# VectorE scales the residual inside the feed-forward and makes the fillers' low parts; block 2's constants are loaded behind its first projections

## The chip, the cores and the metric

The kernel runs on one core of one Trainium2 chip. The core has five engines that each follow their own instruction order and meet at semaphores: TensorE (PE, matrix products into PSUM; PEld is its weight load), VectorE (DVE), ScalarE (ACT), GpSimd (POOL) and SyncE (SP), which here only issues DMA transfers. The metric is the device time of one execution in microseconds, as the median of several runs.

## What is computed

The reference is two transformer blocks in a row on one sequence of 256 latent tokens and 256 context tokens, width 1024, all in float32. Cut to what matters here:

```python
# block 1: layer 0 a gated linear attention (GLA), layer 1 a state-space mixer (SSD)
hl = layer_norm(ALPHA * hl + m_l[2] * mixer(...), ln_g[i, 0], ln_b[i, 0])
hl = layer_norm(ALPHA * hl + m_l[5] * sq_relu_mlp(modulate(hl, m_l[3], m_l[4]), ffn_w1[i], ffn_w2[i]),
                ln_g[i, 1], ln_b[i, 1])       # in layer 0 also for the context rows hc
# sq_relu_mlp(h, w1, w2) = square(relu(h @ w1)) @ w2, d_ff = 4096
# block 2: two layers, each with three attentions on projections of one normed input
h = rms_norm(x, norm_g[l]) * (1 + scale) + shift
(na_q, na_k, na_v, cq, ckv, ..., z, gm) = split(h @ w_in[l])
x = x + gate * merge_branches(neighbourhood, latent, differential attention)
```

In the feed-forward the normed rows are used twice. Its input is modulated from them, with the gain `ln_g` and bias `ln_b` folded into the modulation's columns; its residual needs them with gain and bias applied: `gain` multiplies the rows by `ln_g` and adds `ln_b` in place.

## The kernel before, in words

**Matrix products in three passes.** Float32 operands are split into a high part (type fp32r) and the low remainder. `gemm` walks over units of weights, 128 x 1024 values (512 KB) each, that `unit` loads: SP issues the transfer into `wr` (three buffers), ScalarE casts it to `wh`, and the subtraction `wl = wr - wh` (line 400) gives the low part; `wh` and `wl` have two buffers each. Which engine subtracts is `self.loeng`: VectorE by default. TensorE then does wh times xh, wh times xl and wl times xh for each output tile.

**Norms and fillers.** Tokens go through a norm in pairs of 128-row tiles. `stats` and `norm` run on VectorE (a chain of 128x2 instructions for the reciprocal root, lines 363 to 371), with one of the two rows scaled on ScalarE; `fill_x` transposes the rows on TensorE and splits them to `xh` and `xl`. While a pair is normed, TensorE is given a product that does not need it, a filler. There are six of them with `lo_on(LOENG)`, four units each, so 24 units: the first 256 columns of the feed-forward's first product in layer 0 (`ffn`, q = c = 0); the first product of the SSD for the first 256 tokens (group 0); the context part of block 2's first projection, computed ahead inside block 1's second feed-forward phase (`nak_ctx`); and in block 2 the first two token tiles of the projections `nav` and `naq` (layer 0) and `nak` (layer 1), by `split=True` in `b_in`. `lo_on` sets `self.loeng` for the product inside it, and sets `self.rate`, the pace of background work (the adaptive modulation, whose accumulations `adav` at line 573 run on VectorE), to 0 if the engine is GpSimd and `keep` is not given. The SSD's product for `z` uses `lo_on(SLO, True)` with `SLO = "gpsimd"`, 16 units more; that line is not touched.

**The feed-forward** (`ffn`) runs over four quarters q of d_ff; in each, two products of the first matrix (c = 0, 1) and two of the second, accumulated in `facc`. The residual `h` is read in the sink of the second product at q = 2. A callback `later` is called after the first product of q = 0.

**The residual's scaling** (`gain`, lines 754 to 761) loads the two rows to all partitions (SP, `row`, four buffers) and does two instructions of 128x1024 per tile, on GpSimd by default (`GAINENG`): four tiles in layer 0 from `later`, two in layer 1 directly ahead of `ffn`. With `after=True` the planner may not put the multiply ahead of the last matmul issued so far.

**Block 2's constants** (`b_consts`): four transfers on SP (`gc`, two parts of `gr`, the lambda vectors in a `bsq` buffer), six small VectorE instructions and one exponential on ScalarE, at the start of each layer.

**Order.** The program's planner (the Tile scheduler with its simulated timeline) fixes each engine's order ahead of the run: among the instructions that it takes to be ready, the one that stands first in the program, moved by `prio`. An instruction may be placed long before its place in the program if its buffers are free. On the chip each engine then follows that order.

Of the kernel before, what the change touches and what calls it, by code (L numbers as in the profile page):

```python
# [22 lines left out]
SRATE = 1  # L23
PEY = 4
VSPLIT = (0,)
LOENG = "gpsimd"
TCN = 4
NBRX = 1
GAH = 1
# [241 lines left out]
class K:  # L271
# [505 lines left out]
    def ffn(self, l, h, u, gates, mode, between=None, later=None):  # L777

        nc, A = self.nc, self.A
        nt = len(h)  # L780
        n = nt * P
        acc = [self.t([P, D], "facc", nt) for _ in range(nt)]
        off1 = off2 = 0
        self.rate = FRATE[l]
        self.wprio = FWP[l]
        for q in range(4):
            hx = self.new_x(mode, 8, n)
            if q == 2:
                gates = gates()
            for c in range(2):  # L790
                def sink(p, k, c0, hx=hx):
                    n = p.shape[1]
                    cs = slice(c0, c0 + n)
                    r = self.t([P, 512], "frelu", 2)
                    nc.scalar.activation(out=r[:, :n], in_=p, func=AF.Relu)
                    if mode == "f4":
                        nc.vector.tensor_tensor(out=hx.h[k][:, cs], in0=r[:, :n], in1=p, op=ALU.mult)
                    else:
                        f = self.t([P, 512], "fsq", 2)
                        nc.scalar.activation(out=f[:, :n], in_=r[:, :n], func=AF.Square)  # L800
                        nc.scalar.copy(out=hx.h[k][:, cs], in_=f[:, :n])
                        nc.vector.tensor_tensor(out=hx.l[k][:, cs], in0=f[:, :n], in1=hx.h[k][:, cs].bitcast(F32),
                                                op=ALU.subtract)
                parts = [(0, n)]
                if q == c == 0 and nt == 4:
                    parts = [(0, 256), (256, 256)]
                for c0, m0 in parts:
                    jobs = [("F", m * P, P, c0, m0, (lambda p, k=c * 4 + m: sink(p, k, c0))) for m in range(4)]
                    with self.lo_on(LOENG if len(parts) == 2 and c0 == 0 else "vector"):
                        o = self.gemm(A[f"w1{l}"], off1, KD, 512, u, jobs)  # L810
                off1 = o
                if later is not None and q == c == 0:
                    later()
            for c in range(2):
                if nt == 4 and 2 * q + c >= FSTOP:
                    self.rate = 0

                def sink2(p, t):
                    cs = slice(c * 512, (c + 1) * 512)
                    a = acc[t][:, cs]  # L820
                    if q == 0:
                        nc.scalar.copy(out=a, in_=p)
                    elif q < 3:
                        nc.vector.tensor_tensor(out=a, in0=p, in1=a, op=ALU.add)
                    else:
                        g = self.t([P, 512], "fsq", 2)
                        nc.vector.tensor_tensor(out=g, in0=p, in1=gates[t][:, cs], op=ALU.mult)
                        nc.vector.tensor_tensor(out=a, in0=a, in1=g, op=ALU.add)
                        self.stats(acc, t, c)
                    if q == 2:  # L830
                        nc.vector.tensor_tensor(out=a, in0=a, in1=gates[t][:, cs], op=ALU.mult)
                        nc.vector.scalar_tensor_tensor(out=a, in0=h[t][:, cs], scalar=ALPHA, in1=a,
                                                       op0=ALU.mult, op1=ALU.add)
                jobs = [("T", 0, 512, t * P, P, (lambda p, t=t: sink2(p, t))) for t in range(nt)]
                if q == 3 and c == 1 and between is not None:
                    self.gemm(A[f"w2{l}"], off2, 8, 512, hx, jobs[:2])
                    between(acc)
                    jobs = jobs[2:]
                off2 = self.gemm(A[f"w2{l}"], off2, 8, 512, hx, jobs)
        self.rate = 0  # L840
        self.wprio = WPRIO
        return acc
# [318 lines left out]
    def ssd(self, u, mode):  # L1161
# [29 lines left out]
        for g in range(8):  # L1191
# [21 lines left out]
            if g == 0:  # L1213
                jobs = [("F", j * P, P, 0, 256, (lambda p, j=j: conv(p, j, 0))) for j in range(3)]
                with self.lo_on(LOENG):
                    self.gemm(A["swin"], off, KD, 512, u, jobs)
# [188 lines left out]
    def block1(self, mode="r3", upto=99):  # L1405
        nc, A = self.nc, self.A
# [22 lines left out]
        u = self.new_x(mode, KD, 512)  # L1429
# [8 lines left out]
        am = {}  # L1438
# [16 lines left out]
        with self.phase("ffn0"):  # L1455
            self.floor = 8
            gl, gc = (self.row_load(d, eng=RLQ) for d in rows)
            xt = load_x("H", RLQ)
            sh, sc = am[0, 3], am[0, 4]
            cols = [self.mod_cols(sh[i], sc[i], 0) for i in (1, 0)]  # L1460
            u = self.new_x(mode, KD, 512)
            r = self.out_resid(A["gwout"], KD, og, xt, [gc, gc, gl, gl],
                               between=lambda r: self.norm_pair(u, r, 0, cols[0]))
            self.norm_pair(u, r, 1, cols[1])
            if upto < 1:
                return
            def gates0():
                gl, gc = (self.row_of(am[0, 5][i]) for i in range(2))
                return [gc, gc, gl, gl]
            u1 = self.X2 = X(mode)  # L1470

            def between0(r):
                self.finish(20)
                sh, sc = am[1, 0], am[1, 1]
                self.cols1 = [self.mod_cols(sh[i], sc[i], 1) for i in (1, 0)]
                self.grow_x(u1, KD, 512)
                self.norm_pair(u1, r, 0, self.cols1[0])
            with self.prio(3000):
                self.ctx_norm()
            r = self.ffn(0, r, u, gates0, mode, between0, lambda r=r: self.gain(r, 0, after=True))  # L1480
            u = u1
            self.norm_pair(u, r, 1, self.cols1[1])
            self.finish(8)
            self.floor = 0
            for t in range(2):
                getattr(nc, Q4).dma_start(out=self.hs[t], in_=r[2 + t])
# [5 lines left out]
        with self.phase("ffn1"):  # L1492
# [17 lines left out]
            u = self.new_x(mode, KD, 512)  # L1510
            self.ctx_to_x(u)
            r = self.out_resid(A["swout"], 16, yx, h, [gl, gl], fac)
# [3 lines left out]
            with self.tc.tile_pool(name="xpf", bufs=1, reuse_waits="tile") as self.xp:  # L1516
                sh, sc = am[1, 3], am[1, 4]
                u = self.new_x(mode, KD, 256)
                self.norm_to_x(u, r, [self.mod_cols(sh[0], sc[0], 2)])
                self.gain(r, 2)  # L1520
                for t in range(2):
                    self.dump(f"h3_{t}", r[t])
                r = self.ffn(1, r, u, lambda: [self.row_of(am[1, 5][0])] * 2, mode)
                self.finish(0)
            self.open_xp2()
            u = self.new_x(mode, KD, 512)
# [45 lines left out]
    def nak_ctx(self, u):  # L1572
# [4 lines left out]
        def sink(p, t):  # L1577
            x = self.t([P, 512], "frelu", 2)
            nc.scalar.copy(out=x, in_=p)
            getattr(nc, Q4).dma_start(out=self.nak0[t], in_=x)  # L1580
        with self.lo_on(LOENG):
            self.b_in(0, "nak", range(2), u, sink)
# [60 lines left out]
    def b_in(self, l, name, toks, u, sink, split=False):  # L1643
# [7 lines left out]
        if not split:  # L1651
            return part(toks)
        with self.lo_on(LOENG):
            part(toks[:2])
        return lambda: part(toks[2:])

    @contextmanager
    def lo_on(self, eng, keep=False):

        old = self.loeng, self.rate  # L1660
        self.loeng = eng
        if eng == "gpsimd" and not keep:
            self.rate = 0
        yield
        self.loeng, self.rate = old
# [455 lines left out]
    def block2(self, mode="r3", upto=99):  # L2121
        nc, A = self.nc, self.A
# [3 lines left out]
        if not hasattr(self, "first2"):  # L2126
            self.open_xp2()
            y, u = [self.ty() for _ in range(4)], self.new_x(mode, KD, 512)
# [6 lines left out]
        with self.phase("b2"):  # L2135
# [6 lines left out]
            for l in range(2):  # L2142
                am = self.am2[l]
                toks = range(4) if l == 0 else range(2, 4)
                self.loeng = B2LO[l]
                ntk = len(toks)
                self.b_consts(l)
                y, u = self.first2 if l == 0 else (ynew, unew)
                t0 = toks[0]
                ya, yb = [x[:, 0:512] for x in y], [x[:, 512:1024] for x in y]  # L2150
# [8 lines left out]
                if l == 0:  # L2159
                    rest2, nav = self.b_v(l, "nav", u, split=True)  # L2160
                    rest3, naq = self.b_qk(l, "naq", toks, u, ya[t0:], 0, split=True)
                    rest()
                    rest2()
                    nak = nak()
                    rest3()
                else:
                    rest()
                    nav = self.b_v(l, "nav", u)
                    nak = nak()
                    naq = self.b_qk(l, "naq", toks, u, ya[t0:], 0)  # L2170
# [160 lines left out]
```

## Time and profile before

| | us |
|---|---|
| median of 3 runs | 2514.3 |
| lowest, highest | 2512.57, 2516.8 |
| profiled execution | 2518.34 |
| its span, first to last instruction | 2516.5 |

The granted clock of TensorE in the profiled execution is 0.973 of full speed on average. PE, DVE, ACT and POOL in the rows are TensorE, VectorE, ScalarE and GpSimd; an engine's busy time does not say whether an instruction was held up while it ran. In a window, PEclk is the mean granted clock of TensorE, 1.00 for 2.4 GHz. The span runs from block 1's GLA over its first feed-forward (from about 405), the SSD (from about 810) and the second feed-forward (from about 1220) to block 2's layer 0 (from about 1436) and layer 1 (from about 2080).

### The profile page before, as it was taken

Reading aid. Unit: us, or ns where it says so; the run is one execution under the profiler, and the core shown is the slowest. Engines: PE = TensorE matmul, PEld = TensorE weight load, DVE = VectorE, ACT = ScalarE, POOL = GpSimd, SP = SyncE. Lnnn points to the kernel's source line nnn. Section 1 sums busy time; section 2 is a strip of 40 time slices with the busy share of each in tenths; the row PEclk is TensorE's granted clock in tenths of the full one; section 3 lists DMA queues with packets and bytes.
Section 4 is the critical chain, followed back from the end, with each engine's and each line's share of the span. In section 5 each row is a group of like instructions: output and inputs, shape, how many; then the busy total and the mean of one; then the engine's idle time right before and its main releaser. Section 6 shows DMA issues by size and latency. Waiting matters only on the chain.

```text
span 2516.5 us, 36824 instructions
## 1 busy us (share of the span) xinstructions
PE 2394.9 (95%) x13879; PEld 1917.3 (76%) x13879; DVE 1741.8 (69%) x3320; ACT 1210.5 (48%) x2367; POOL 363.0 (14%) x308
## 2 busy tenths in 40 slices
PE   7999998999999899999899989999999998999998
PEld 4777766777776777877688868788777877877776
DVE  3455578966588867687765676986555566798676
ACT  3445544432323455565565455554444345564553
POOL 0011113100000134443310120100011001100020
PEclk8999998999999899999999999999999999999999
DMA  6322245555655444523565552222122354333354
GB/s 252 101 77 85 77 148 179 192 200 207 205 199 181 156 161 141 178 84 109 163 209 185 184 172 86 81 80 74 61 92 64 111 168 141 121 111 99 104 154 138
DMA packets 105394, 348.01 MB, mean 138 GB/s; under 512 B 14200, under 2 KB 20288, under 8 KB 105216
## 3 DMA queue, kind: packets, MB, share of 16 engines
q1 hardware_dynamic: 100304, 333.22, 40.4%
q0 software_dynamic: 3616, 12.06, 1.4%
q8 instruction: 109, 1.79, 0.3%
q14 instruction: 69, 0.57, 0.1%
q10 hardware_dynamic: 1296, 0.38, 0.1%
HBM read 338.75 MB, written 6.85 MB: 137 GB/s over the span
## 4 chain that ended last, share of the span: by engine, by line
PE 47%; DVE 3%; ACT 1%; issue 1%; DMA 1%; POOL 0%; SPq 0%; DVEq 0%; POOLq 0%; ACTq 0%
PE acc L439 39%; PE ps L1728 3%; PE ps L1756 2%; PE aps L1867 1%; PE ps L1640 1%; PE aps L1772 1%; DVE wl L400 1%; PE acc L1640 0%; PE ps L741 0%; DMA row<-rowd 0%; DMA bsq<-in_gr 0%; ACT wh L395 0%; DVE xl L751 0%; DVE xl L1718 0%; DVE yacc L1382 0%
## 5 line engine op out<-in xcount | busy, mean ns | idle before, releaser
L395 ACT CAST wh<-wr 128x1024 fp32r<-128x1024 f32 (+3 forms) x461 | 472.5, 1027 | 638.7 <-PE acc L439 557.7
L439 PE MATMUL acc<-wh,xh 128*128 128x512 f32 (+3 forms) x1876 | 727.4, 394 | 12.2 <-ACT wh L395 6.3
L400 DVE TENSOR_TENSOR wl<-wr,wh 128x1024 fp32r<-128x1024 f32 (+3 forms) x421 | 519.2, 1235 | 314.0 <-ACT wh L395 235.4
L439 PE MATMUL acc<-wh,xl 128*128 128x512 f32 (+3 forms) x1876 | 720.4, 388 | 6.7 <-DVE xl L1570 6.4
L439 PE MATMUL acc<-wl,xh 128*128 128x512 f32 (+3 forms) x1876 | 508.0, 387 | 5.8 <-POOL wl L400 4.0
L439 PEld LDWEIGHTS acc<-wh,xh 128*128 128x128 f32 x1876 | 358.3, 192 | 96.7 <-ACT wh L395 12.9
L439 PEld LDWEIGHTS acc<-wh,xl 128*128 128x128 f32 x1876 | 358.5, 192 | 80.6 <-DVE xl L1570 7.7
L439 PEld LDWEIGHTS acc<-wl,xh 128*128 128x128 f32 x1876 | 343.6, 190 | 84.6 <-POOL wl L400 6.2
L439 PE MATMUL acc<-xh,wh 128*128 128x512 f32 (+2 forms) x1024 | 344.3, 353 | 3.8 <-ACT wh L395 2.3
L439 PE MATMUL acc<-xl,wh 128*128 128x512 f32 (+2 forms) x1024 | 340.3, 348 | 7.5 <-DVE xl L751 7.5
L439 PE MATMUL acc<-xh,wl 128*128 128x512 f32 (+1 forms) x1024 | 232.2, 347 | 3.3 <-DVE wl L400 3.3
L439 PEld LDWEIGHTS acc<-xh,wh 128*128 128x128 f32 (+1 forms) x1024 | 196.0, 193 | 38.4 <-issue 6.7
L439 PEld LDWEIGHTS acc<-xl,wh 128*128 128x128 f32 (+1 forms) x1024 | 196.9, 193 | 33.1 <-DVE xl L751 8.8
L400 POOL TENSOR_TENSOR wl<-wr,wh 128x1024 fp32r<-128x1024 f32 x40 | 97.9, 2448 | 720.8 <-ACT wh L395 630.9
L439 PEld LDWEIGHTS acc<-xh,wl 128*128 128x128 f32 x1024 | 167.2, 191 | 36.3 <-issue 6.4
L573 DVE SCALAR_TENSOR_TENSOR adav<-wrd,s,adav 128x512 f32<-128x512 f32 x196 | 146.7, 780 | 53.0 <-DMA wrd<-in_ada 52.0
L1742 ACT ACTIVATE bP<-ps,bnm 128x512 f32<-128x512 f32 (+1 forms) x144 | 88.5, 621 | 86.5 <-DVE bnm L1739 71.4
L2003 POOL TENSOR_SCALAR bP<-bP,brc 128x512 f32<-128x512 f32 (+1 forms) x24 | 33.4, 1396 | 488.2 <-DVE brc L2000 467.5
L1739 DVE TENSOR_REDUCE bnm<-ps 128x1 f32<-128x512 f32 (+1 forms) x120 | 78.2, 684 | 32.3 <-PE ps L1728 32.0
L1204 DVE SCALAR_TENSOR_TENSOR scv<-acc,scw,scv 128x510 f32<-128x510 f32 (+3 forms) x140 | 83.6, 635 | 14.7 <-ACT scv L1200 14.4
L1756 PE MATMUL ps<-ident,bP 128*128 128x128 f32 x400 | 60.3, 277 | 2.5 <-ACT bPT L1631 1.4
L1631 ACT COPY bPT<-ps 128x512 f32<-128x512 f32 x75 | 43.9, 595 | 33.9 <-PE ps L1756 27.9
(430 smaller groups left out, 3100.4 us busy)
## 6 DMA issues: line engine op xcount, KB each, us to landing
wr<-in_w SPq DMA_DIRECT2D x136, 512.0 KB, 3.6
wr<-in_win SPq DMA_DIRECT2D x136, 512.0 KB, 3.6
wrd<-in_ada SPq DMA_DIRECT2D x128, 512.0 KB, 4.4
wr<-in_swin SPq DMA_DIRECT2D x52, 512.0 KB, 3.6
wr<-in_gwin SPq DMA_DIRECT2D x24, 512.0 KB, 3.4
wr<-in_wbr SPq DMA_DIRECT2D x24, 512.0 KB, 3.4
wr<-in_wout SPq DMA_DIRECT2D x24, 512.0 KB, 3.8
wst<-in_ada SPq DMA_DIRECT2D x16, 512.0 KB, 7.3
```

The source lines that it names most:

```text
L395: nc.scalar.copy(out=hi[:, :n], in_=raw[:, :n])
L400: getattr(nc, eng).tensor_tensor(out=lo[:, :n], in0=raw[:, :n], in1=hi[:, :n].bitcast(F32), op=ALU.subtract)
L439: mm = nc.tensor.matmul(out=o, lhsT=wv if kind == "F" else xv, rhs=xv if kind == "F" else wv, start=b["first"], stop=bool(fin and b["left" ...
L573: o = nc.vector.scalar_tensor_tensor(out=a, in0=xi, scalar=c, in1=a, op0=ALU.mult, op1=ALU.add)
L1204: nc.vector.scalar_tensor_tensor(out=c[:, :, o0:o1], in0=pv[:, :, i0:i1], scalar=w[:, tap:tap + 1], in1=c[:, :, o0:o1], op0=ALU.mult, op1= ...
L1631: return self.nc.scalar.copy(out=out, in_=in_)
L1640: nc.tensor.transpose(p[:width, t * P:(t + 1) * P], x[:, j * width:(j + 1) * width], self.ident)
L1728: mms.append(self.nc.tensor.matmul(out=p[:, n * nk:(n + 1) * nk], lhsT=q[a][rows, i * P:(i + 1) * P], rhs=k[b][rows, :nk], start=m == 0, s ...
L1739: nc.vector.tensor_reduce(out=nm[:, :n], in_=p.rearrange("p (n k) -> p n k", n=n), axis=AX.X, op=ALU.max, negate=True)
L1742: nc.scalar.activation(out=e[:, i * nk:(i + 1) * nk], in_=p[:, i * nk:(i + 1) * nk], func=AF.Exp, bias=nm[:, i:i + 1], accum_out=sm[i])
L1756: mms.append(nc.tensor.transpose(p[:, d:d + P], e[:, c:c + P], self.ident))
L2003: nc.gpsimd.tensor_scalar(out=b, in0=b, scalar1=rc[:, 1, i:i + 1], scalar2=None, op0=ALU.mult)
```

## The change

Three edits. `LOENG` becomes "vector", so that the 24 filler units have their low part made by VectorE; `lo_on` now sets the rate to 0 whenever `keep` is not given, and `ffn` passes `keep` for all of its products but the first, so that the rates are those of before. The callback `later` is called at q = 1, c = 0 instead of q = c = 0, and both feed-forwards pass `gain` on VectorE as that callback; in layer 1 it stood ahead of `ffn`. `b_consts` moves from the start of each block-2 layer to a place behind the rest of the projection `nak` (layer 1), or of `nak` and `nav` (layer 0).

```diff
--- before.py
+++ after.py
@@ -23,7 +23,7 @@
 SRATE = 1
 PEY = 4
 VSPLIT = (0,)
-LOENG = "gpsimd"
+LOENG = "vector"
 TCN = 4
 NBRX = 1
 GAH = 1
@@ -806,10 +806,10 @@
                     parts = [(0, 256), (256, 256)]
                 for c0, m0 in parts:
                     jobs = [("F", m * P, P, c0, m0, (lambda p, k=c * 4 + m: sink(p, k, c0))) for m in range(4)]
-                    with self.lo_on(LOENG if len(parts) == 2 and c0 == 0 else "vector"):
+                    with self.lo_on(LOENG, len(parts) == 1 or c0 > 0):
                         o = self.gemm(A[f"w1{l}"], off1, KD, 512, u, jobs)
                 off1 = o
-                if later is not None and q == c == 0:
+                if later is not None and q == 1 and c == 0:
                     later()
             for c in range(2):
                 if nt == 4 and 2 * q + c >= FSTOP:
@@ -1477,7 +1477,7 @@
                 self.norm_pair(u1, r, 0, self.cols1[0])
             with self.prio(3000):
                 self.ctx_norm()
-            r = self.ffn(0, r, u, gates0, mode, between0, lambda r=r: self.gain(r, 0, after=True))
+            r = self.ffn(0, r, u, gates0, mode, between0, lambda r=r: self.gain(r, 0, nc.vector, True))
             u = u1
             self.norm_pair(u, r, 1, self.cols1[1])
             self.finish(8)
@@ -1517,10 +1517,8 @@
                 sh, sc = am[1, 3], am[1, 4]
                 u = self.new_x(mode, KD, 256)
                 self.norm_to_x(u, r, [self.mod_cols(sh[0], sc[0], 2)])
-                self.gain(r, 2)
-                for t in range(2):
-                    self.dump(f"h3_{t}", r[t])
-                r = self.ffn(1, r, u, lambda: [self.row_of(am[1, 5][0])] * 2, mode)
+                r = self.ffn(1, r, u, lambda: [self.row_of(am[1, 5][0])] * 2, mode,
+                             later=lambda r=r: self.gain(r, 2, nc.vector, True))
                 self.finish(0)
             self.open_xp2()
             u = self.new_x(mode, KD, 512)
@@ -1659,7 +1657,7 @@
 
         old = self.loeng, self.rate
         self.loeng = eng
-        if eng == "gpsimd" and not keep:
+        if not keep:
             self.rate = 0
         yield
         self.loeng, self.rate = old
@@ -2144,7 +2142,6 @@
                 toks = range(4) if l == 0 else range(2, 4)
                 self.loeng = B2LO[l]
                 ntk = len(toks)
-                self.b_consts(l)
                 y, u = self.first2 if l == 0 else (ynew, unew)
                 t0 = toks[0]
                 ya, yb = [x[:, 0:512] for x in y], [x[:, 512:1024] for x in y]
@@ -2161,10 +2158,12 @@
                     rest3, naq = self.b_qk(l, "naq", toks, u, ya[t0:], 0, split=True)
                     rest()
                     rest2()
+                    self.b_consts(l)
                     nak = nak()
                     rest3()
                 else:
                     rest()
+                    self.b_consts(l)
                     nav = self.b_v(l, "nav", u)
                     nak = nak()
                     naq = self.b_qk(l, "naq", toks, u, ya[t0:], 0)
```

## Rows read from the trace of the kernel before

**Rows 1.** Page, part 1: the span; busy us, share and instructions of each engine.

```profile
span 2516.5 us, 36824 instructions
PE 2394.9 (95%) x13879; PEld 1917.3 (76%) x13879; DVE 1741.8 (69%) x3320; ACT 1210.5 (48%) x2367; POOL 363.0 (14%) x308
```

**Rows 2.** GpSimd's groups by shape: count, busy us, mean ns, idle before and its releasers.

```profile
L400 POOL TENSOR_TENSOR wl<-wr,wh 128x1024 fp32r<-128x1024 f32 x40 | 97.9, 2448 | 720.8 <-ACT wh L395 630.9 <-PE acc L439 81.5 <-issue 8.0
...
L761 POOL TENSOR_TENSOR yacc<-yacc,row 128x1024 f32<-128x1024 f32 x6 | 17.7, 2983 | 0.0
...
L758 POOL TENSOR_TENSOR yacc<-yacc,row 128x1024 f32<-128x1024 f32 x6 | 15.1, 2540 | 18.8 <-PE ps L741 18.8
```

**Rows 3.** VectorE's groups by shape, the costliest, with the same columns.

```profile
L400 DVE TENSOR_TENSOR wl<-wr,wh 128x1024 fp32r<-128x1024 f32 x392 | 498.1, 1272 | 294.5 <-ACT wh L395 223.7 <-PE acc L439 55.5 <-ACT bsq L2019 5.3
```

**Rows 4.** Source line 758, its VectorE instructions: ns min, median, max, first and last start.

```profile
L758 DVE TENSOR_TENSOR by<-by,row x2: 1218/1222/1226, 1450.2 to 1451.4; 128x1024 f32<-128x1024 f32 x2
```

**Rows 5.** Windows, seven stretches and one for comparison; the first line names the columns.

```profile
core 0: us, PE busy (x) PEld busy (x) DVE busy (x) ACT busy (x) POOL busy (x), PEclk, DMA share, GB/s
404.00:436.00 32.00, 26.18 (x174) 24.20 (x173) 29.32 (x50) 17.74 (x36) 16.21 (x7) 0.84 0.45 149
436.00:458.00 22.00, 14.33 (x70) 12.06 (x69) 22.00 (x18) 8.06 (x19) 15.88 (x6) 0.77 0.33 107
809.00:850.00 41.00, 26.44 (x150) 22.36 (x149) 33.52 (x87) 18.31 (x33) 10.92 (x6) 0.74 0.36 119
1220.00:1248.00 28.00, 19.34 (x74) 13.64 (x73) 21.11 (x47) 12.10 (x18) 10.06 (x5) 0.94 0.56 193
1248.00:1270.00 22.00, 18.14 (x125) 17.27 (x125) 20.09 (x21) 13.09 (x29) 11.33 (x5) 0.84 0.52 169
1436.00:1492.00 56.00, 45.07 (x180) 33.80 (x179) 42.35 (x72) 28.30 (x47) 25.62 (x14) 0.91 0.54 180
2080.00:2120.00 40.00, 33.36 (x140) 25.97 (x139) 28.00 (x47) 23.90 (x45) 10.68 (x6) 0.87 0.44 143
2040.00:2080.00 40.00, 39.31 (x177) 31.25 (x176) 29.21 (x47) 21.46 (x33) 3.26 (x6) 1.00 0.73 229
```

**Rows 6.** Timeline of VectorE: start us, us, instruction, shape, count, idle before if any.

```profile
419.09 2.27 DVE L365 TENSOR_SCALAR rsqy<-rsqy 128x2 int32<-128x2 int32 x1
...
446.82 5.60 DVE L573 SCALAR_TENSOR_TENSOR adav<-wrd,s,adav 128x512 f32<-128x512 f32 x2
...
812.47 2.28 DVE L369 TENSOR_TENSOR rsqw<-rsqy 128x2 f32<-128x2 f32 x1
...
823.16 0.15 DVE L369 TENSOR_TENSOR rsqw<-rsqy 128x2 f32<-128x2 f32 x1
...
1226.92 3.49 DVE L1382 SCALAR_TENSOR_TENSOR yacc<-wrd,yacc 128x512 f32<-128x512 f32 x2
...
1263.03 3.39 DVE L400 TENSOR_TENSOR wl<-wr,wh 128x1024 fp32r<-128x1024 f32 x1
...
1452.49 6.72 DVE L761 TENSOR_TENSOR by<-by,row 128x1024 f32<-128x1024 f32 x2
...
2062.80 1.29 DVE L2239 TENSOR_TENSOR by<-by,bo 128x512 f32<-128x512 f32 x2
...
2086.22 3.16 DVE L2239 TENSOR_TENSOR by<-by,bo 128x512 f32<-128x512 f32 x2
```

**Rows 7.** Timeline of TensorE, two starts after a wait, with the wait in brackets.

```profile
821.65 1.92 PE L586 MATMUL aps<-adav,one 128*32 128x512 f32 x4 [9.48 <-DVE adav L573]
...
2103.88 1.54 PE L741 MATMUL ps<-ident,by 128*128 128x128 f32 x6 [4.15 <-ACT by L1624]
```

**Rows 8.** Windows inside the two feed-forwards, columns as in the windows above.

```profile
540.00:560.00 20.00, 20.00 (x90) 15.16 (x89) 15.61 (x23) 8.36 (x17) 0.00 (x0) 1.00 0.59 201
1310.00:1330.00 20.00, 20.00 (x149) 19.04 (x148) 11.05 (x15) 14.30 (x32) 0.00 (x0) 1.00 0.62 184
```

**Rows 9.** Timeline of SyncE's queue: one transfer of the constants of block 2's layer 1.

```profile
1968.08 0.33 SPq L2107 DMA_DIRECT2D bsq<-in_gr  x1
```

## The prediction

> **What bounds the kernel now.** The page first [rows 1]: TensorE is busy 2394.9 of 2516.5 us, so nothing gains unless it lets TensorE wait less or run at its upper clock; VectorE at 69% and GpSimd (POOL) at 14% matter only where TensorE waits for them. The groups of GpSimd come next [rows 2]: what the change takes from it is 40 low parts minus the 16 that the variable `SLO` keeps, so 24 of 2.45 us, and the scalings of the residual, six multiplies of 2.54 and six additions of 2.98 us. GpSimd has time for both, and TensorE hardly waits for it by name.
>
> The windows say where the time goes [rows 5]. A stretch's loss is its length less TensorE's busy time times the granted clock. It is 10.0 us in 404 to 436, 11.0 in 436 to 458, 21.4 in 809 to 850, 9.8 in 1220 to 1248, 6.8 in 1248 to 1270, 15.0 in 1436 to 1492 and 11.0 in 2080 to 2120, 85 us together. The 24 low parts and the 12 scalings all run in these seven stretches: each is a norm whose latency TensorE bridges with fillers, four units of weights (eight in 1436 to 1492). The stretch 2040 to 2080 is a norm of the same kind, whose fillers' low parts VectorE makes already: TensorE is busy 39.31 of 40 us at full clock.
>
> VectorE's timeline shows the mechanism [rows 6]. Two 128x512 additions take 1.29 us at 2062.80 and 3.16 at 2086.22, while GpSimd makes a low part. An instruction on 128x2 takes 0.15 us at 823.16, 2.28 at 812.47 beside a low part, and 2.27 at 419.09 beside a scaling. So a GpSimd instruction holds VectorE up for most of its own length, in the chain that TensorE waits for: 4.15 us at 2103.88 for the normed rows, 9.48 at 821.65 behind an accumulation of VectorE [rows 7].
>
> The Trainium skill, "SBUF — State Buffer", section "Who interferes with whom", says that the two engines share a port pair by an exclusive lock, held for the whole instruction. By that alone the 36 instructions could block VectorE for 24 x 2.45 + 6 x 2.54 + 6 x 2.98 = 92 us, an estimate; the timeline has 60.6, as VectorE is not always due, and the sum uses that.
>
> **Blocked time, by stretch.** I add what VectorE's instructions took beyond the same shape unblocked; one row of each stretch stands [rows 6]. 404 to 436: six instructions, 9.4 us (5.1 by low parts, 4.3 by scalings). 436 to 458: six, 12.4, all scalings. 809 to 850: three, 7.9. 1220 to 1248: three, 4.5. 1248 to 1270: four, 8.2, all scalings. 1436 to 1492: four, 11.1, where the two additions at 1452.49 alone took 6.72 against 2 x 1.22 [rows 4]. 2080 to 2120: four, 7.1. Low parts block 35.7 us, scalings 24.9.
>
> **Low parts.** 24 go to VectorE at 1.22 us (the unblocked length; the group's mean of 1.27 has blocked ones in it [rows 3]): 29.3 us more work, 35.7 less blocking, a net of only 6.4. Behind a waiting low part on VectorE stand the norm and, behind that, ScalarE's cast of the next weights and TensorE. The mean idle time before a low part is 294.5/392 = 0.75 us [rows 3], mostly where VectorE has nothing else to do; in the norm at 2040 to 2080 the loss is 0.7 us in all, low parts included [rows 5]. Ends: nothing added where VectorE idles, -35.7; every low part waiting 0.75, 29.3 + 18.0 - 35.7 = +11.6. I take the value near the net, as that stretch is the nearest case. GpSimd's remaining work does not shrink: the low parts of `SLO` and the bias additions still block where they stand. The rates of the background work stay as they were, as `lo_on` now sets them to 0 by `keep` and the callers pass it to match.
>
> **Residual scaling, first feed-forward.** Eight instructions leave GpSimd and come back on VectorE at 1.22 us [rows 4], 9.8 us, a pass of weights later (q = 1, c = 0), near 550 us. There TensorE is busy 20.00 of 20 us and VectorE 15.61 [rows 8], so the work fits on average; in one burst it can hold up a low part. 20.00/90 x 24 matmuls make a unit of 5.3 us, one unit is ahead, so a burst costs at most 9.8 - 5.3 = 4.5 us, once. **Second feed-forward:** four instructions, 4.9 us, from just before to q = 1, c = 0, near 1320; VectorE has 11.05 of 20 us there and TensorE waits for nothing [rows 8]. 20.00/149 x 24 = 3.2 us a unit, so at most 1.7. Both: 0 to 6.2 us, I take 2, as other instructions can come in between. The four row loads on SP (512 KB each) move back as well; they stay far ahead of their use and the row buffers suffice, so I give them 0, with 1 us either way where they stand among weight loads. The result is read at q = 2, two gemms later.
>
> **Block 2's constants.** Four transfers, six small VectorE instructions and one ScalarE exponential per layer are placed behind the first projections. The planner issues them when a queue is idle: layer 1's constants were issued at 1968.08 [rows 9], over 100 us before that layer began. So the move may do nothing; layer 0's leave the norm at best. What can go is under 1 us of unblocked instructions, with SP's four issues of 0.43 us up to 3. Their use is tens of us later, behind the projections; no loss.
>
> **Sum.** What reaches TensorE, by stretch: 404 to 436, 9.4 - 4.9 = 4.5. 436 to 458, 12.4 blocked but only 11.0 lost, and VectorE is full there without it (22.00 of 22): 9. 809 to 850, 7.9 - 4.9 = 3.0: 2, since the 9.48 us wait is for an accumulation behind the norm. 1220 to 1248, 4.5 - 4.9: 0. 1248 to 1270, 8.2 blocked, 6.8 lost: 6. 1436 to 1492, 11.1 - 9.8 = 1.3, and with the constants and the low parts that fall before the norm: 3. 2080 to 2120, 7.1 - 4.9 = 2.2, and by its twin at 2040: 3. Together 27.5, less 2 for the bursts: 25.5. The profiled execution took 2518.3 us, so 2492.8; it stands 4.0 above the median of the runs (2514.3), which gives 2489 us.
>
> **Rivals.** A: this forecast, 15 to 40 us less. 0.60.
>
> B: low parts wait in VectorE's queue. If the planner's order has them before their weights are cast, each adds the 0.75 us of the group [rows 3], 18 us: -25.5 + 18 = -7.5, 2507 us. For it: that mean; against: the stretch at 2040. 0.15.
>
> C: more comes back. Idle and lost clock feed each other: in 436 to 458 the clock is 0.77 [rows 5], TensorE at its lower level (1.2 GHz) for part of it right after waits. If half of the 85 us returns, 2472 us. 0.08.
>
> D: no change, within 0.2% (5 us, about what a measurement of this kernel can tell): moving work between two engines that block each other gains nothing, and the planner's new order costs what the scalings give. By rows: low parts +11.6, scalings -17 (three stretches at 4.3, 9 and 6 less 2): -6, about 2509; 2514 with 5 us of order lost. The Trainium skill, "Perfetto Trace Analysis", section "Optimizing Scalar/DVE Operations", says that offloading between these two might not help as they share a read port; the trace bears it out for the low parts (net 6.4 of 60.6), not for the scalings, which go where VectorE idles. 0.10.
>
> E: slower. One mechanism: VectorE works in order, and a low part that stands before a norm's instruction holds it until TensorE frees the weight buffer, one filler unit earlier. From a mean wait of 25.5/24 = 1.1 us per low part the gain is gone; at 1.5 us it is 36 - 25.5 = 10.5 us slower, 2525. For it: a filler unit outlasts that wait; against: rows 5 at 2040 again, and that TensorE has fillers while VectorE waits. 0.07.
>
> **Numbers.** Faster A, B and C, 0.83; same D, 0.10; slower E, 0.07. The range 2470 to 2510 holds A, B, most of C and the near half of D; the ends of the terms (-35.7 - 21.6 - 3, and +11.6 + 6.2) go beyond it on both sides, but would all have to fall together.
>
> **What would show it.** GpSimd's group of low parts has 16 instead of 40, with no multiply or addition of rows on yacc, and VectorE's low parts grow to 416 (of 128x1024). In the seven stretches VectorE's 128x2 instructions take under 0.2 us; TensorE's waits after 436 and at 1263 are gone, and the clock is higher there. The twelve scalings stand near 550 and 1320, and TensorE stays 20 of 20 us busy around them. Wrong would be: a low part on VectorE waiting over 1 us inside a norm, TensorE idle around 550, or new waits in block 2 behind another order. The largest term, 436 to 458, fails if TensorE there waits for VectorE's accumulations anyway.

## The result, and the profile after

The changed kernel takes 2486.69 us (median of 4 runs, 2483.96 to 2490.76), the one before 2513.44 us beside it (median of 4): ratio 0.9894, 95% interval [0.9878, 0.9909], so 23 to 31 us less. Forecast were 2489 us, in 2470 to 2510. The profiled execution took 2490.76 us against 2518.34.

The page of the changed kernel, to be read against [rows 1], then its groups of low parts by shape, against [rows 2, 3]:

```profile
span 2489.0 us, 36804 instructions
PE 2382.5 (96%) x13879; PEld 1908.7 (77%) x13879; DVE 1725.9 (69%) x3356; ACT 1210.8 (49%) x2367; POOL 271.5 (11%) x272
```

```profile
L400 POOL TENSOR_TENSOR wl<-wr,wh 128x1024 fp32r<-128x1024 f32 x16 | 38.1, 2381 | 86.9 <-PE acc L439 72.2 <-ACT wh L395 14.7
...
L400 DVE TENSOR_TENSOR wl<-wr,wh 128x1024 fp32r<-128x1024 f32 x416 | 519.8, 1252 | 298.2 <-ACT wh L395 234.2 <-PE acc L439 42.0 <-ACT xtmp L921 6.8
```

GpSimd loses 24 low parts and all twelve scalings. VectorE has 36 instructions more and is busy 15.9 us less: 36 at 1.22 us, 43.9, came, so by this sum 59.8 us of held-up time went, against the 60.6 that the prediction counted. Windows of the changed kernel, to be read against [rows 5] (the third and fourth at the same work, 22 and 26 us earlier; the fifth around the first scalings, against [rows 8]), and VectorE's timeline of those scalings:

```profile
404.00:433.00 29.00, 24.06 (x170) 22.80 (x169) 23.77 (x53) 18.24 (x35) 0.00 (x0) 0.88 0.52 165
433.00:458.00 25.00, 24.47 (x133) 19.91 (x133) 24.56 (x51) 12.98 (x27) 0.00 (x0) 1.00 0.66 232
...
1226.00:1248.00 22.00, 21.17 (x151) 19.35 (x151) 14.87 (x27) 16.46 (x35) 1.14 (x2) 0.96 0.57 190
...
2054.00:2092.00 38.00, 33.23 (x150) 26.58 (x149) 27.48 (x54) 26.64 (x48) 1.08 (x2) 0.96 0.52 168
530.00:552.00 22.00, 22.00 (x95) 16.83 (x94) 21.72 (x26) 10.80 (x17) 0.00 (x0) 1.00 0.60 198
```

```profile
534.05 4.62 DVE L758 TENSOR_TENSOR yacc<-yacc,row 128x1024 f32<-128x1024 f32 x4
538.59 1.41 DVE L573 SCALAR_TENSOR_TENSOR adav<-wrd,s,adav 128x512 f32<-128x512 f32 x2
539.91 3.49 DVE L761 TENSOR_TENSOR yacc<-yacc,row 128x1024 f32<-128x1024 f32 x3
```

Behind 433 us TensorE is busy 24.47 of 25 us at the upper clock (2.4 GHz), where before it was 14.33 of 22 at 0.77. In the feed-forward VectorE is full for a while (21.72 of 22 us) and TensorE does not notice.

Both traces have 13879 matmuls, so one can ask how much earlier the matmul with the same number starts. That gives the gain of each stretch (times of before; worked out from the starts of the matmuls at both ends of it; us):

```
stretch        forecast  changed   the stretch is
404 to 436        4.5      2.6     norm, low parts and scalings
436 to 458        9       11.5     norm, scalings
809 to 855        2        5.5     norm, low parts
855 to 1220       0       -2.2     SSD stage, nothing of it edited
1220 to 1270      6        5.7     norm, low parts, then scalings
1436 to 1492      3        2.9     norm, low parts, constants
2080 to 2120      3        4.4     norm, low parts
498 to 776       -2       -0.6     first feed-forward, burst of scalings
2120 to the end   0       -2.4     block 2, layer 1
```

The -2 was forecast for the bursts of both feed-forwards; the second shows -0.1. The rest is under 1 us a line. The stretches of the edit gave 32.6 us, 5 of them went again elsewhere, 27.6 are left in these two traces. The -0.6 is not the burst's: it stands in the traces of the runs below that leave the scalings on GpSimd beside the norms and move the low parts of the first feed-forward's head, and it is 0.0 where the scalings alone are moved.

### The profile page after: what moved, and what is told of

The parts are those of the page before. It is cut to its first block, busy times and chain, and to the rows that moved or that the text cites. A ratio compares the mean times of both kernels' runs of the same rounds, so it can differ in the third digit from the quotient of the medians.

```text
span 2489.0 us, 36804 instructions
## 1 busy us (share of the span) xinstructions
PE 2382.5 (96%) x13879; PEld 1908.7 (77%) x13879; DVE 1725.9 (69%) x3356; ACT 1210.8 (49%) x2367; POOL 271.5 (11%) x272
## 5 line engine op out<-in xcount | busy, mean ns | idle before, releaser
L400 DVE TENSOR_TENSOR wl<-wr,wh 128x1024 fp32r<-128x1024 f32 (+4 forms) x445 | 540.8, 1217 | 318.2 <-ACT wh L395 246.6
L573 DVE SCALAR_TENSOR_TENSOR adav<-wrd,s,adav 128x512 f32<-128x512 f32 x196 | 140.3, 747 | 44.8 <-DMA wrd<-in_ada 43.5
L1754 PEld LDWEIGHTS ps<-ident,bP 128*128 128x128 f32 x400 | 45.9, 140 | 16.5 <-issue 5.9
```

Source lines behind the costliest of these rows:

```text
L400: getattr(nc, eng).tensor_tensor(out=lo[:, :n], in0=raw[:, :n], in1=hi[:, :n].bitcast(F32), op=ALU.subtract)
L573: o = nc.vector.scalar_tensor_tensor(out=a, in0=xi, scalar=c, in1=a, op0=ALU.mult, op1=ALU.add)
L1754: mms.append(nc.tensor.transpose(p[:, d:d + P], e[:, c:c + P], self.ident))
```

## The experiments

The theory: a GpSimd instruction holds VectorE up, and what counts is whether TensorE waits for VectorE at that time; the scalings are the larger part. One rival the trace of before settles: ScalarE, which casts the weights, is not held. Its casts of line 395 take 1.05 us in the median beside GpSimd's 128x1024 instructions (20 of them) and 1.05 elsewhere (412). Differences in us below are medians against the kernel before on the same chip; ratios have 95% intervals.

**One part at a time.** First the scalings alone:

```diff
-                if later is not None and q == c == 0:
+                if later is not None and q == 1 and c == 0:
...
-            r = self.ffn(0, r, u, gates0, mode, between0, lambda r=r: self.gain(r, 0, after=True))
+            r = self.ffn(0, r, u, gates0, mode, between0, lambda r=r: self.gain(r, 0, nc.vector, True))
...
-                self.gain(r, 2)
...
+                             later=lambda r=r: self.gain(r, 2, nc.vector, True))
```

> Theory (GpSimd's long instructions hold VectorE up inside the norms that TensorE waits for, and the scalings are the larger part that reaches TensorE): with the scaling edit alone the stretches 436 to 458 and 1248 to 1270 lose their TensorE waits, 404 to 436 gains some, 809 to 850, 1220 to 1248, 1436 to 1492 and 2080 to 2120 stay as before. By the terms 4.3 + 9 + 6 less 2 that is 17 us, 15 to 20 us faster than before. Rival 1 (the low parts carry the gain, since they were most of the blocked time, 35.7 of 60.6 us): 5 to 10 us faster. Rival 2 (the gain is that of a luckier order of the planner as a whole, not the sum of the parts): no fixed number, but the parts alone would not add up to the 27 us of the whole.

2491.49 us, ratio 0.9903 [0.9884, 0.9923], 22.4 us less. The gain falls where the theory had it and is larger than its price: 404 to 458 gains 15.9 us and 1203 to 1273 6.5. Rival 1 is out. So is rival 2 for the first of these: from 404 to 498 TensorE, VectorE and ScalarE do the same instructions in the same order as before. The complement is the whole change without those lines. What it still has, in part:

```diff
-LOENG = "gpsimd"
+LOENG = "vector"
...
-                self.b_consts(l)
...
+                    self.b_consts(l)
```

> The low parts on VectorE and the moved constants, with the scalings on GpSimd at their old places. Theory: 809 to 850 and 2080 to 2120 gain what they gained in the changed kernel (5.6 and 4.3 us), 1436 to 1492 some 3, the stretches beside scalings little, and block 2's other order takes some 2 back: 6 to 12 us faster than before. Rival 1 (low parts carry the gain): 17 us or more. Rival 3 (low parts are neutral, since 24 of 1.22 us come onto VectorE and net out the blocking): within 4 us of before.

2510.24 us, 0.9978 [0.9966, 0.9990], 3.6 us less. Here 776 to 853 gains 5.6, 1203 to 1273 2.8, 1436 to 1492 3.2 and 2080 to 2120 3.5, but the SSD stage (853 to 1203) gives back 6.9 and 404 to 498 loses 2.0. With the 22.4 that is 26.0 of the 26.75 us: the parts add up, against rival 2 of the run before. Then the constants alone:

```diff
-                self.b_consts(l)
                 y, u = self.first2 if l == 0 else (ynew, unew)
...
                     rest2()
+                    self.b_consts(l)
...
                     rest()
+                    self.b_consts(l)
```

> Only the constants of block 2 are placed behind the first projections. Theory: they were issued ahead of need before, so no change, within 1.5 us. Rival: their four issues and seven small instructions stood in the norm of 1436 to 1492, and the move is the 3 us gained there: 2 to 4 us faster.

2514.16 us, 0.9999 [0.9985, 1.0013]: nothing. The rival is out: 1436 to 1492 loses 0.3, so the 2.9 us there are the low parts'.

**Place or engine.** The changed kernel (lines with - are its own from here on) with the late scalings on GpSimd:

```diff
-... lambda r=r: self.gain(r, 0, nc.vector, True))
+... lambda r=r: self.gain(r, 0, nc.gpsimd, True))
...
-                             later=lambda r=r: self.gain(r, 2, nc.vector, True))
+                             later=lambda r=r: self.gain(r, 2, nc.gpsimd, True))
```

> The changed kernel with the scalings at their new, later places, but on GpSimd. It tells the place from the engine. Theory (what cost time was GpSimd's instructions beside the norm; any place where TensorE has work does): as fast as the changed kernel, within 3 us, so 24 to 30 us faster than before; VectorE's instructions beside the scalings in the feed-forward are held up by about 2 us each and TensorE does not notice. Rival (the engine matters: twelve GpSimd instructions of 2.5 to 3.0 us, 33 us together, hold up VectorE's low parts in the feed-forward, where VectorE is 15.6 of 20 us busy): 5 us or more of the gain is lost, 22 us faster than before or less.

2510.53 us, 0.9984 [0.9971, 0.9997], only 3.3 us less. That looks like the rival, but its timelines of GpSimd, and of TensorE beside it, show something else:

```profile
405.29 5.76 POOL L758 TENSOR_TENSOR yacc<-yacc,row 128x1024 f32<-128x1024 f32 x2 [51.34 <-PE ps L741]
431.85 5.16 POOL L758 TENSOR_TENSOR yacc<-yacc,row 128x1024 f32<-128x1024 f32 x2 [20.81 <-PE ps L741]
436.98 11.11 POOL L761 TENSOR_TENSOR yacc<-yacc,row 128x1024 f32<-128x1024 f32 x4
```

```profile
443.38 0.58 PE L439 MATMUL acc<-xl,wh 128*128 128x256 f32 x1 [8.02 <-DVE xl L751]
```

The scalings did not move. GpSimd has an otherwise empty queue there and starts what its data allow, at 405 and 432 us; a later line in the program, and an order kept only within the planner, hold nothing back. So the run doesn't tell place from engine. It shows again what the old place costs: TensorE waits 8.02 us for an `xl` that VectorE makes beside them. The next run holds them truly, by one instruction ahead in GpSimd's queue, beside that edit (a dependency within the planner keeps the scalings behind it):

```diff
                 if later is not None and q == 1 and c == 0:
+                    z = self.t([P, 512], "frelu", 2)[:, :2]
+                    self.hold = nc.gpsimd.tensor_copy(out=z, in_=hx.h[3][:, 0:2].bitcast(F32))
                     later()
```

> The changed kernel with the scalings on GpSimd, and held to their new place this time: ahead of them GpSimd copies two columns of a tile that the feed-forward's second part makes (into a spare tile), and its queue runs in order. Theory 1 (the place is what counts: beside the norm a held-up VectorE is what TensorE waits for, in the feed-forward it is not): 20 to 27 us faster than before, the norms as in the changed kernel. Theory 2 (the engine counts as well: beside 22 us of GpSimd work near 540 VectorE gets one instruction done for each of GpSimd's, 8 where it has 25 due, and falls 11 us behind, more than the 5 us that a unit of weights is ahead): 5 to 12 us are lost in the first feed-forward, fewer in the second, 10 to 18 us faster than before.

2500.12 us, 0.9928 [0.9912, 0.9944], 16.3 us less: theory 2. The norms gain as in the changed kernel (404 to 458: 14.1 us), and 498 to 776 loses 12.6. The window, then the timelines of GpSimd, VectorE and TensorE around the scalings (line 763 is line 761 of the other kernels):

```profile
540.00:560.00 20.00, 14.22 (x54) 9.90 (x52) 17.68 (x11) 4.73 (x6) 16.44 (x7) 0.87 0.30 106
```

```profile
544.15 10.72 POOL L758 TENSOR_TENSOR yacc<-yacc,row 128x1024 f32<-128x1024 f32 x4
554.83 11.98 POOL L763 TENSOR_TENSOR yacc<-yacc,row 128x1024 f32<-128x1024 f32 x4
```

```profile
545.72 6.95 DVE L573 SCALAR_TENSOR_TENSOR adav<-wrd,s,adav 128x512 f32<-128x512 f32 x3 [1.57 <-DMA wrd<-in_ada]
552.59 3.35 DVE L400 TENSOR_TENSOR wl<-wr,wh 128x1024 fp32r<-128x1024 f32 x1
555.87 2.86 DVE L573 SCALAR_TENSOR_TENSOR adav<-wrd,s,adav 128x512 f32<-128x512 f32 x1
558.65 2.57 DVE L571 TENSOR_SCALAR adav<-wrd,s 128x512 f32<-128x512 f32 x1
561.14 3.41 DVE L400 TENSOR_TENSOR wl<-wr,wh 128x1024 fp32r<-128x1024 f32 x1
```

```profile
556.00 2.93 PE L439 MATMUL acc<-xh,wl 128*128 128x512 f32 x6 [5.78 <-DVE wl L400]
```

From 545.72 to 564.55 us VectorE finishes seven instructions, 2.3 to 3.4 us each, about a GpSimd instruction's length. The low parts of the weights come late, and TensorE waits 5.78 us for one; its granted clock in the window is 0.87, where it was 1.00. Even where VectorE has some 4 of 20 us to spare [rows 8], GpSimd is the dear engine for this. The mirror of it, VectorE at the old places:

```diff
-                if later is not None and q == 1 and c == 0:
+                if later is not None and q == c == 0:
...
+                self.gain(r, 2, nc.vector)
...
-                             later=lambda r=r: self.gain(r, 2, nc.vector, True))
```

> The changed kernel with the scalings on VectorE but written at their old places (behind the first gemm of the first feed-forward, and ahead of the second). Theory (a VectorE instruction there costs the norm its own 1.22 us, not the 2 to 3 us of a held-up one): 12 of 1.22 are 14.6 us, of which some fall into VectorE's idle time, so 5 to 12 us of the gain are lost: 14 to 21 us faster than before. Rival (only the engine counts, VectorE's queue has room): as the changed kernel, within 3 us. Rival (only the place counts): 2 to 7 us faster than before, as with GpSimd.

2489.61 us, 0.9893 [0.9875, 0.9912]: as the changed kernel, 2489.39 us beside it. My theory's 5 to 12 us are not there; the first rival is right. The scalings ran beside the norm, and TensorE stayed busy (VectorE's timeline of the first four, then the window):

```profile
440.90 4.62 DVE L758 TENSOR_TENSOR yacc<-yacc,row 128x1024 f32<-128x1024 f32 x4
```

```profile
433.00:458.00 25.00, 23.66 (x122) 19.22 (x121) 25.00 (x37) 12.04 (x26) 0.00 (x0) 1.00 0.49 164
```

VectorE is full for all 25 us, and background accumulations give way: 11 `adav` instructions of line 573 start in it instead of the changed kernel's 21, the rest later. 404 to 498 gains 11.7 instead of 14.7 us, and the first feed-forward then gains another 1.1.

**What VectorE takes on.** The scalings on GpSimd at the old places, and at the new ones twelve VectorE instructions of the same shape that leave the residual as it is:

```diff
+    def idle_work(self, r):
+        for x in r:
+            for _ in range(2):
+                o = self.nc.vector.tensor_tensor(out=x, in0=x, in1=x, op=ALU.max)
+                self.not_before(o)
```

> The changed kernel with the scalings on GpSimd at their old places, beside the norms, and with twelve VectorE instructions of the same shape at the new places that leave the residual as it is (the larger of x and x). It splits the scaling edit into what leaves GpSimd and what VectorE takes on. Theory (the whole gain is what leaves GpSimd, the twelve VectorE instructions are covered by TensorE's full queue): as with the scalings left where they were, 2510 us, 2 to 7 us faster than before. Rival (VectorE's twelve instructions cost up to 4.5 + 1.7 us in bursts, so the removal is worth more than was seen): 2514 to 2518 us.

2510.06 us, 0.9973 [0.9961, 0.9984], 6.4 us less, no slower than without them (3.6 us less, on another chip). The first eight ran from 548.75 to 559.84 us, and the window there:

```profile
545.00:565.00 20.00, 20.00 (x86) 15.24 (x85) 19.51 (x23) 10.82 (x17) 0.00 (x0) 1.00 0.57 180
```

The bursts cost nothing that can be measured. Four runs on one chip, this one among them, give the whole table, in us less than before: GpSimd at the old places 6.4 (this run, with the twelve idle instructions), GpSimd at the new ones 16.3, VectorE at the old 26.8, VectorE at the new 27.0. The engine is worth 20 us at the old places and 11 at the new; the place is worth 10 on GpSimd and nothing on VectorE.

**Single low parts, and noise.** The changed kernel again:

> The changed kernel once more, on the chip of the runs beside it, as their yardstick: 2486.7 us, 25 to 29 us faster than before.

2489.39 us, 0.9885 [0.9864, 0.9905]. Its stretches gain 5.8 (776 to 853), 5.3 (1203 to 1273) and 4.3 us (2080 to 2120), but the SSD stage gives back 4.6 instead of 2.5, and at 404 us this execution is 7 us ahead of the first one of the same program, at its end 1. So much in a single profile's stretch is accident.

The traces also say how far the SSD stage's loss is one of order. In the runs with the scalings alone and with the constants alone, TensorE, VectorE and ScalarE have the order of the kernel before in 853 to 1203; the one loses 3.4 us there all the same, the other gains 3.0. In the seven traces with the changed kernel's order it loses 1.0 to 6.9. The cost of the order shows best in 880 to 950: 4.9 to 11.0 us in those seven, 0.0 and 1.6 in the two. A part comes back behind it, and what the order costs in the whole stage can't be told from one trace. Then the low parts of the SSD stage on VectorE too:

```diff
-SLO = "gpsimd"
+SLO = "vector"
```

> The changed kernel with the last 16 low parts, those of the SSD stage, on VectorE as well. Theory (a low part that moves frees VectorE of about what it costs, 1.22 us on it against some 1.5 us of blocking in a norm, and the SSD stage has other GpSimd work, which stays): no change against the changed kernel, within 4 us; by the low parts' price here (24 of them and the constants gave 3.6 us) 2 us faster. Rival (VectorE is 16 to 22 of 25 us busy in the SSD stage, and its queue holds a low part in front of the scan's own steps): 4 to 10 us slower than the changed kernel.

2495.03 us, 0.9919 [0.9901, 0.9937], 21 us less than before where the changed kernel had 27. By medians that is the rival, some 6 us slower; but the changed kernel was not run on this chip, the interval of its second set of runs, [0.9864, 0.9905], overlaps a little with this one, and the profile, that of the fastest run (2489.13 us), shows no place for a loss. It stays open. Next the four low parts of the first feed-forward's head back on GpSimd:

```diff
-                    with self.lo_on(LOENG, len(parts) == 1 or c0 > 0):
+                    with self.lo_on("gpsimd" if len(parts) == 2 and c0 == 0 else "vector", len(parts) == 1 or c0 > 0):
```

> The changed kernel with the low parts of the first feed-forward's head alone, four units near 404 to 420, back on GpSimd. In the run with the scaling edit alone, where they were on GpSimd, the stretch 404 to 497 gained 17.5 us, against 14.2 in the changed kernel. Theory (there the low parts stand between the norm's 128x2 steps in VectorE's queue and cost what their blocking did, so the place decides for each filler): 2 to 4 us faster than the changed kernel. Rival (the difference of two runs was an accident of a transfer, and four low parts are 5 us on either engine): within 1.5 us of the changed kernel.

2494.66 us, 0.9919 [0.9903, 0.9935], on the same chip: 5 us slower by medians, again at the edge of what the intervals tell apart. The theory's gain is not there in the whole. In the edited stretch it is: 16.5 us gained from 404 to 498 against 14.7. TensorE's first wait for the normed rows there, before, in the changed kernel and in this one:

```profile
424.65 1.54 PE L741 MATMUL ps<-ident,yacc 128*128 128x128 f32 x6 [5.28 <-ACT yacc L723]
```

```profile
424.49 2.46 PE L741 MATMUL ps<-ident,yacc 128*128 128x128 f32 x10 [4.94 <-ACT yacc L723]
```

```profile
420.36 0.87 PE L741 MATMUL ps<-ident,yacc 128*128 128x128 f32 x6 [1.04 <-ACT yacc L723]
```

But 776 to 853 gains 2.7 less, and the SSD stage gives back 10.2 us. Nothing was edited there; the planner's queues for it came out in another order, but this profile is also that of the slowest of six runs (2500.95 us), so how much of it is the order's stays open. The mirror, these four alone on VectorE, on the kernel before:

```diff
-                    with self.lo_on(LOENG if len(parts) == 2 and c0 == 0 else "vector"):
+                    with self.lo_on("vector", len(parts) == 1 or c0 > 0):
...
-        if eng == "gpsimd" and not keep:
+        if not keep:
```

> The mirror of the run before it: the kernel before with the four low parts of the first feed-forward's head alone on VectorE, all else as it was. The changed kernel with these four on GpSimd was 5 to 8 us slower than the changed kernel, and none of that fell in the stretch beside them; it fell between 809 and 1270. Theory (what four low parts give beside the norm is about nothing, 5.1 us of blocking against 4 of 1.22 us; the 5 to 8 us are the queues' new order in the SSD stage, which comes out differently for every edit ahead of it): stretch 404 to 497 within 2 us of before, and the whole within 4 us of before, with a shift of either sign in the SSD stage. Rival (these four low parts are worth 5 to 8 us wherever the time shows): 5 to 8 us faster than before.

2514.87 us, 1.0007 [0.9996, 1.0018], 377 to 498 gains 1.1: beside GpSimd's scalings these four are worth nothing, as the theory had it. Last, the four low parts of the SSD stage's first projection back on GpSimd, in the changed kernel:

```diff
-                with self.lo_on(LOENG):
+                with self.lo_on("gpsimd"):
                     self.gemm(A["swin"], off, KD, 512, u, jobs)
```

> The changed kernel with the four low parts of the SSD stage's first projection alone back on GpSimd. The changed kernel gained 5.7 us in 809 to 855, where 2 had been counted on; the run with the scaling edit alone gained 2.4 there. Theory (these low parts blocked the norm ahead of the SSD stage, and the loss was half idle time and half clock, so taking 7.9 us of blocking away gives more than the 3 us net): the stretch loses 3 to 4 us again, and the whole is 2 to 5 us slower than the changed kernel. Rival (the stretch's gain is one of order): the stretch keeps its 5 us.

2488.19 us, 0.9903 [0.9886, 0.9919]. The stretch (776 to 853) is 7.3 us worse, more than the theory said, and the SSD stage behind it, in another order, gains 3 to 5 of these back. The whole is 2 us slower by medians, which the intervals don't tell from nothing. The rival is out for the stretch. TensorE's timeline in this kernel, then in the changed one ([rows 7] has 9.48 for before):

```profile
805.44 1.92 PE L586 MATMUL aps<-adav,one 128*32 128x512 f32 x4 [9.47 <-DVE adav L573]
...
822.22 0.39 PE L439 MATMUL acc<-xl,wh 128*128 128x256 f32 x1 [1.76 <-DVE xl L751]
```

```profile
805.73 1.92 PE L586 MATMUL aps<-adav,one 128*32 128x512 f32 x4 [7.37 <-DVE adav L573]
```

No version beat the changed kernel; the one with VectorE at the old places equals it.

## Why the prediction was right, point by point

- **The mechanism** held. The chain of 128x2 instructions of the changed kernel, in VectorE's timeline beside four low parts on VectorE (against 2.27 and 2.28 in [rows 6]):

```profile
418.18 0.17 DVE L363 TENSOR_SCALAR rsqy<-lnv 128x2 int32<-128x2 int32 x1
418.38 0.17 DVE L365 TENSOR_SCALAR rsqy<-rsqy 128x2 int32<-128x2 int32 x1
...
420.50 1.22 DVE L400 TENSOR_TENSOR wl<-wr,wh 128x1024 fp32r<-128x1024 f32 x1 [0.58 <-ACT wh L395]
421.64 0.15 DVE L370 TENSOR_TENSOR rsqw<-rsqw,lnv 128x2 f32<-128x2 f32 x1
```

- **404 to 436** was mis-sized: 4.5 forecast, 2.6 measured. The rows above show why: a low part stands inside the chain, with a wait of 0.58 us and 1.22 of its own, and the norm ends at 424 us as before (TensorE's wait there is 4.94 us, against 5.28). Where the scalings are gone and these low parts stay on GpSimd, the stretch gains 4.4 us (scalings alone) and 5.4 (the head's low parts put back) and the wait is 1.04. So the whole gain there is the scalings', and the four low parts cost some 2 us of it.
- **436 to 458**, the largest term, was 9 and gave 11.5: I took off 2 because VectorE is full there. It is full without the scalings as well (24.56 of 25 us), but with background work that can wait, and the granted clock comes back from 0.77 to 1.00.
- **The scalings** were 17 and measured 22.4, interval 19 to 29 less by the ratio: 404 to 458 gains 15.9 where 13.3 was reckoned, and the bursts cost nothing where 2 was taken.
- **Low parts and constants** were 8.5 and measured 3.6 by medians (2.5 to 8.5 less by the ratio). Behind the first feed-forward they gave more than forecast: in the three runs with the low parts moved and GpSimd's scalings beside the norms, 776 to 853 gains 4.9 to 5.6 against 2. I had taken off 1 because TensorE's wait there was for an accumulation behind the norm; that accumulation stood behind held-up instructions itself, and in the changed kernel the wait falls from 9.48 to 7.37 us. The other 3 us come later in the stretch, at a granted clock that the sum had no term for. Windows of about the same work, before and then in the changed kernel:

```profile
844.00:855.00 11.00, 8.88 (x49) 8.12 (x50) 5.35 (x13) 3.48 (x9) 0.00 (x0) 0.69 0.51 172
```

```profile
828.00:836.00 8.00, 6.66 (x53) 5.92 (x53) 5.53 (x15) 3.32 (x9) 0.00 (x0) 1.00 0.51 181
```

  The sum also had no term for the new order, which goes with the SSD stage's loss of 1.0 to 6.9 us in single traces.
- **The constants** came out at nothing, as said.
- **Rival B** fell as a whole: the idle time before a low part is 298.2/416 = 0.72 us, against 0.75 before, and no norm but that of 404 to 436 shows its cost. C fell, 27 us came back and not 42. E fell: in the changed kernel no stretch of a norm became slower.
- **Rival D** named the Trainium skill, "Perfetto Trace Analysis", section "Optimizing Scalar/DVE Operations", by which moving work between these engines might not help. The runs split it: for the 24 low parts it nearly holds (3.6 us less), for the twelve scalings it doesn't (22.4 us less), and it makes no difference where VectorE does them (26.8 and 27.0 us less in the whole). A likely reason, not tested by itself: nobody waits for a scaling until the feed-forward's third part (q = 2), so it can stand in VectorE's queue, where a low part is wanted at once. That they had to go where VectorE idles, as the prediction put it, is wrong.

So the total was right partly by luck, because two errors took each other out: by medians the scalings were forecast 5 us too low and the low parts 5 too high. The first is clear of the noise; the second is not quite, as the interval for the low parts ends at the 8.5 us that were forecast.

## What to carry to other kernels

Price a GpSimd instruction of this kind at its own length in VectorE time, wherever VectorE has instructions with two SBUF inputs to do, and compare that with what the same instruction takes on VectorE; spare time on GpSimd is not free. Where an engine's queue is empty, a later line in the program delays nothing: only data or an instruction ahead in that queue does. Sum by stretch, look at the clock of each stretch as well as at its waits, and allow several us in stretches that the edit doesn't touch, for a new order of the planned queues and for accident: here a stage moved by 3 us either way with its order unchanged.

## What was not expected of the hardware

Not every VectorE instruction is held up. In VectorE's timeline of the kernel before, beside GpSimd instructions that run from 413.86 to 416.67 and from 434.60 to 451.88 us:

```profile
414.33 1.27 DVE L703 BATCH_NORM_STATS2 lnst<-yacc 128x6 f32<-128x512 f32 x2
...
441.01 0.53 DVE L745 TENSOR_SCALAR xtmp<-ps,mcs,mcb 128x256 f32<-128x256 f32 x1
441.46 2.13 DVE L751 TENSOR_TENSOR xl<-xtmp,xh 128x256 fp32r<-128x256 f32 x1
```

The statistics (one input from SBUF) take 0.64 us each, and the multiply-add that reads PSUM 0.53, their usual lengths; the subtraction of two SBUF tiles takes 2.13 instead of 0.42. That is the Trainium skill's rule in "SBUF — State Buffer", section "Who interferes with whom": VectorE with at most one SBUF input, outside its two-port modes, doesn't contend with GpSimd. The trace agrees. The one-input multiply at 558.65 us in the held run took 2.57 instead of 0.48; whether it ran in a two-port mode no row shows. The 92 us of blocking that the prediction estimated by that page were too many for this reason too: the page makes this exception, and it names the hold for the whole instruction with VectorE's two-port modes.

GpSimd pays as well, though less: its held scalings took 10.72/4 = 2.68 and 11.98/4 = 3.00 us beside VectorE's work. With no VectorE instruction beside it, a low part of the same shape takes it 2.38 us (at 888.70 in the changed kernel).
